# Grid attention in a hybrid diffusion layer: scores, exponentials and scaling as three background steps, and a new order of the steps

## The chip, the cores and the metric

The kernel runs on one core of one Trainium2 chip. The core has a matrix engine (PE, with its weight loads shown apart as PEld), a vector engine (DVE), an activation engine (ACT), a general engine (POOL) and a queue that issues transfers (SP). Each engine works through its own instructions in the order in which the program lists them, and the engines wait for each other on semaphores. The metric is the device time of one execution in microseconds.

## The reference

One layer over 512 latent tokens (an 8 x 64 grid) and 256 context tokens of width 1024. A combined input projection feeds three mixers (a short convolution, a gated linear recurrence, and a neighbourhood attention over the grid), which are merged, projected and followed by a mixture of 16 experts. The change is in the neighbourhood attention, which the reference writes, cut to its core, as

```
s_loc = einsum('bnqhd,bwnkhd->bhnqwk', qr, kr) * scale + bias       # keys of the window
s_ctx = einsum('bnqhd,blhd->bhnql', qr, kc) * scale                 # 256 context keys
p = softmax(concatenate([s_loc, s_ctx], -1), -1)
o = einsum('bhnqwk,bwnkhd->bnqhd', p_loc, vr) + einsum('bhnql,blhd->bnqhd', p_ctx, vc)
```

There are 8 heads and 4 blocks of 16 grid columns. For one head and one block there are 128 queries (8 rows x 16 columns) and 512 keys (256 of the grid, with masked ones at a large negative bias, and 256 of the context).

## The kernel before

**Stages.** The time is spent in a modulation and input projection with the recurrence (to about 386 us), a stage in which the attention is worked off beside the last input projections (about 386 to 561 us), the merge of the branches (561 to 738), the output projection and the router (738 to 828), and the experts, whose 384 MB of weights are streamed from main memory (from 828 to the end).

**The attention is background work.** In its stage the foreground is a list of 128 projection steps of three matmuls each (L453: 128 x 512 outputs, into three PSUM banks named `pj`), and three steps that transpose the last values (`v_rows`, L862 and L868). `weave(fg, bg)` runs the foreground list and after each of its steps takes as many background steps as keep the two lists in proportion by cost. The order of the program is the order of issue: it is written out by hand, and nothing reorders it later. The background list is `att_bg`; an entry `None` is an empty step that only takes its share of the spacing.

**Pairs.** The work is cut into 16 pairs n (a pair of heads, a block of columns); u = 0 and 1 are the two heads. The steps of a pair are:

- `att_scores(n)`: matmuls of queries with grid keys and context keys into two PSUM banks named `hg`, one for each head (L894; there are two such banks in all). On DVE the bias is added (L897) and the maximum of each row is taken (L898). On ACT the exponential with its row sum is taken from PSUM into a buffer `g` in SBUF (L900). In every fourth pair it also issues the three transfers of the next heads' bias (L880).
- `att_scale(n)`: on DVE a reciprocal of the row sum (L908) and the scaling of the probabilities in place (L909).
- `att_turn(n, u)`: four transposes of the scaled probabilities on PE into the one PSUM bank named `tp` (L917), and their copy to SBUF on ACT (L919). The next transposes into `tp` have to wait for that copy.
- `att_values(n)`: matmuls of values with turned probabilities into a bank `acc` (L934); after every fourth pair ACT and DVE split the result into a rounded part and a rest (L939, L940).

**Other work on ACT and DVE.** Each foreground step group also brings casts and differences that split the next weights (L366 on ACT, L367 on DVE), copies out of the `pj` banks (L956 and L994 on ACT), the convolution (L962 to L967 on DVE) and splits of its results (L554, L555). They stand in the same queues.

The list before takes per pair, in this order, values of n-1, scaling of n, scores of n+1 with their exponentials, and the two turns of n.

Of the kernel before, what the change touches and what calls it, by code (L numbers as in the profile page):

```python
# [14 lines left out]
AF = mybir.ActivationFunctionType  # L15
# [131 lines left out]
def mixer_moe(ctx: ExitStack, tc: tile.TileContext, a, out):  # L147
    nc = tc.nc
    V, S, G, PE, SP = nc.vector, nc.scalar, nc.gpsimd, nc.tensor, nc.sync
# [8 lines left out]
    def bank(tag):  # L158
        return psum.tile([128, 512], F32, tag=tag, name=tag, bufs=pbufs[tag])
# [8 lines left out]
    def g512(dt=F32):  # L168
        return gen.tile([128, 512], dt, tag="g", name="g", bufs=NA_)
# [705 lines left out]
    ast = {}  # L875

    def att_load(hp):
        for t in range(3):
            b_ = gen.tile([128, 2, 256], F32, tag="bias", name="bias", bufs=4)
            SP.dma_start(out=b_, in_=a["bias"][2 * hp:2 * hp + 2, :, 256 * t:256 * t + 256].rearrange("u p k -> p u k"))  # L880
            ast["b", hp, t] = b_

    def att_scores(n):
        def f():
            hp, cb = au[n]
            if cb == 3 and hp < 3:
                att_load(hp + 1)
            rs = [slice(64 * u, 64 * u + 64) for u in range(2)]
            ps = [bank("hg") for _ in range(2)]
            qs = nq[hp][:, 128 * cb:128 * cb + 128]  # L890
            for c, keys in enumerate((nk[hp][:, 64 * KB0[cb]:64 * KB0[cb] + 256],
                                      nkc[hp // 2][:, 256 * (hp % 2):256 * (hp % 2) + 256])):
                for u in range(2):
                    PE.matmul(ps[u][:, 256 * c:256 * c + 256], qs[rs[u]], keys[rs[u]], start=True, stop=True)  # L894
            for u in range(2):
                st_ = gen.tile([128, 4], F32, tag="st", name="st", bufs=4)
                V.tensor_tensor(ps[u][:, 0:256], ps[u][:, 0:256], ast["b", hp, BTYPE[cb]][:, u], op=ALU.add)  # L897
                V.tensor_reduce(st_[:, 0:1], ps[u], axis=AX.X, op=ALU.max, negate=True)  # L898
                p = g512()
                S.activation(p, ps[u], AF.Exp, bias=st_[:, 0:1], accum_out=st_[:, 1:2])  # L900
                ast["p", n, u] = (p, st_)
        return f

    def att_scale(n):
        def f():
            for u in range(2):
                p, st_ = ast["p", n, u]
                V.reciprocal(st_[:, 2:3], st_[:, 1:2])  # L908
                V.tensor_scalar(p, p, st_[:, 2:3], None, op0=ALU.mult)  # L909
        return f  # L910

    def att_turn(n, u):
        def f():
            p, _ = ast["p", n, u]
            pt = bank("tp")
            for c in range(4):
                PE.transpose(pt[:, 128 * c:128 * c + 128], p[:, 128 * c:128 * c + 128], ident)  # L917
            pT = g512()
            S.copy(pT, pt)  # L919
            ast["t", n, u] = pT  # L920
            del ast["p", n, u]
        return f

    def att_values(n):
        def f():
            hp, cb = au[n]
            pT = [ast.pop(("t", n, u)) for u in range(2)]
            if cb == 0:
                ast["o"] = bank("acc")
            po = ast["o"]  # L930
            vs = (nv["lat"][:, KB0[cb]], nv["lat"][:, KB0[cb] + 2], nv["ctx"][:, 0], nv["ctx"][:, 1])
            for c in range(4):
                for u in range(2):
                    PE.matmul(po[64 * u:64 * u + 64, 128 * cb:128 * cb + 128],  # L934
                              vs[c][:, 128 * hp + 64 * u:128 * hp + 64 * u + 64],
                              pT[u][:, 128 * c:128 * c + 128], start=(c == 0), stop=(c == 3))
            if cb == 3:
                hi, lo = g512(F32R), g512(F32R)
                S.copy(nat_q(hi), perm_q(po))  # L939
                V.tensor_tensor(nat_q(lo), perm_q(po), nat_q(hi.bitcast(F32)), op=ALU.subtract)  # L940
                yv[2][hp] = (hi, lo)
        return f

    att_bg = [att_scores(0)]
    for n in range(16):
        att_bg += [att_values(n - 1) if n else None, att_scale(n), att_scores(n + 1) if n < 15 else None,
                   att_turn(n, 0), att_turn(n, 1)]
    att_bg += [None, att_values(15)]


    cst = {}
# [172 lines left out]
    for pr in range(2):  # L1124
        for i in (2 * pr, 2 * pr + 1):
            n = 16 + 3 * pr + (i % 2)
            fg += use_item(n, [proj(n, 0, ev_c(i)), proj(n, 1, ev_u(i))])
        n = 18 + 3 * pr
# [371 lines left out]
```

## Time and profile before

| what | us |
|---|---|
| three runs, median (lowest to highest) | 1747.03 (1745.23 to 1747.78) |
| the profiled execution's own time | 1746.03 |
| its span in the trace | 1744.0 |
| attention stage, as the windows below cut it | 174.70 |
| PE busy in it | 154.31 |
| DVE and ACT busy in it | 90.99 and 68.88 |

Four views are read. The windows give each engine's busy time in a stretch, with the clock that PE was granted (1.00 is 2.4 GHz, 0.50 is 1.2 GHz) and the share of time in which the transfer engines were busy. The waits say who stood idle for whom, in total, how often, and the longest. The timeline lists instructions in order of time; a bracket behind one is the idle time of its engine before it and what ended that. The list of transfers gives their size and time to landing. PE's ends are modelled and a new matmul may start before the modelled end of the last one, so distances between starts are read rather than durations.

### The profile page before, as it was taken

To read this page: it belongs to the slowest core of one execution; us is meant where nothing else is said; L and a number is where in the kernel's file an instruction comes from. 1 tells how busy PE (TensorE), PEld (TensorE's weight loads), DVE (VectorE), ACT (ScalarE), POOL (GpSimd) and SP (SyncE) were. 2 spreads that over 40 slices of the span, in tenths; PEclk is the share of its full clock that TensorE was granted. 3 is DMA by queue.
4 is the path that set the end of the run, shared out by engine and by line. 5 is a ranking of instruction groups with operands and counts; after the bars stand their busy time and mean duration, and the time that the engine had idled before them with its cause. 6 is when DMAs were issued, how large, how long until landed. Compare 5 with 4: busy or idle time off the path is not lost.

```text
span 1744.0 us, 20473 instructions
## 1 busy us (share of the span) xinstructions
PE 1616.1 (93%) x8382; PEld 904.6 (52%) x8382; DVE 569.3 (33%) x1135; ACT 369.5 (21%) x759; POOL 79.6 (5%) x150
## 2 busy tenths in 40 slices
PE   4999999998889999999999999898899998989988
PEld 2767888776666888896343342242322322423322
DVE  3518776435554343334012111121121111201211
ACT  3414445333444232323000000000000000000000
POOL 0314330000000000000000000000000000000000
PEclk8999999999999999998999999999999999999999
DMA  9860112111111332355999999999999999999997
GB/s 343 277 245 25 49 49 73 49 67 67 67 61 43 109 133 106 140 226 223 408 426 426 427 426 426 427 427 427 427 426 427 426 427 427 426 427 426 427 426 321
DMA packets 80745, 487.77 MB, mean 280 GB/s; under 512 B 8972, under 2 KB 12556, under 8 KB 25740
## 3 DMA queue, kind: packets, MB, share of 16 engines
q1 hardware_dynamic: 80652, 486.47, 68.3%
q8 instruction: 66, 1.08, 0.2%
q14 instruction: 27, 0.22, 0.0%
HBM read 484.34 MB, written 2.10 MB: 279 GB/s over the span
## 4 chain that ended last, share of the span: by engine, by line
PE 44%; DMA 38%; DVE 6%; ACT 2%; issue 1%; SPq 0%; ACTq 0%; DVEq 0%
PE pj L453 17%; DMA W<-in_w_exp_dram 12%; DMA B<-in_w_exp_dram 9%; PE pj L1365 7%; DMA A<-in_w_exp_dram 7%; DMA D<-in_w_exp_dram 6%; DMA C<-in_w_exp_dram 4%; PE pj L1016 4%; PE acc L1392 3%; PE pj L1197 3%; PE hg L1333 1%; DVE st L898 1%; PE hg L724 1%; PE acc L1437 1%; PE hg L1422 1%
## 5 line engine op out<-in xcount | busy, mean ns | idle before, releaser
L453 PE MATMUL pj<-A,W 128*128 128x512 f32 x1536 | 410.8, 406 | 2.9 <-ACT W L366 1.9
L453 PEld LDWEIGHTS pj<-A,W 128*128 128x128 f32 x1536 | 275.9, 191 | 72.8 <-issue 21.4
L367 DVE TENSOR_TENSOR W<-W 128x512 fp32r<-128x512 f32 (+1 forms) x184 | 122.3, 688 | 166.6 <-ACT W L366 166.4
L1365 PE MATMUL pj<-W,xe 128*64 128x512 f32 x688 | 159.0, 599 | 8.4 <-DMA W<-in_w_exp_dram 8.4
L1425 DVE TENSOR_TENSOR acc<-acc,hg 128x512 f32<-128x512 f32 x120 | 77.1, 684 | 219.2 <-PE hg L1422 219.2
L1372 ACT ACTIVATE s<-pj 128x512 f32<-128x512 f32 x32 | 19.1, 597 | 513.7 <-PE pj L1365 513.7
L1365 PE MATMUL pj<-A,xe 128*64 128x512 f32 x512 | 118.5, 599 | 6.7 <-DMA A<-in_w_exp_dram 6.7
L1365 PE MATMUL pj<-B,xe 128*64 128x512 f32 x432 | 101.3, 599 | 4.2 <-DMA B<-in_w_exp_dram 4.2
L1365 PEld LDWEIGHTS pj<-W,xe 128*64 128x64 f32 x688 | 45.6, 136 | 113.5 <-issue 84.1
L366 ACT CAST W<-W 128x512 fp32r<-128x512 f32 (+1 forms) x184 | 103.3, 599 | 0.0
L1374 DVE TENSOR_TENSOR s<-s,pj 128x512 f32<-128x512 f32 x32 | 21.9, 684 | 231.7 <-PE pj L1365 231.7
L1392 PE MATMUL acc<-W,at 128*64 128x512 f32 x320 | 74.0, 600 | 9.5 <-DMA W<-in_w_exp_dram 9.4
L1413 DVE TENSOR_TENSOR ye<-mod,acc 64x512 f32<-64x512 f32 x30 | 20.6, 686 | 187.0 <-PE acc L1392 186.5
L1365 PEld LDWEIGHTS pj<-A,xe 128*64 128x64 f32 x512 | 33.6, 136 | 83.6 <-issue 62.3
L1382 ACT COPY at<-tp 128x512 f32<-128x512 f32 x32 | 18.8, 586 | 254.8 <-PE tp L1380 254.2
L1422 PE MATMUL hg<-ye,oht 64*128 64x512 f32 x240 | 67.7, 641 | 0.0
L1365 PEld LDWEIGHTS pj<-B,xe 128*64 128x64 f32 x432 | 28.5, 136 | 69.8 <-issue 54.5
L1392 PE MATMUL acc<-B,at 128*64 128x512 f32 x240 | 56.5, 600 | 8.0 <-DMA B<-in_w_exp_dram 8.0
L453 PEld LDWEIGHTS pj<-C,W 128*128 128x128 f32 x384 | 59.0, 190 | 9.1 <-ACT y L625 0.8
L1365 PE MATMUL pj<-C,xe 128*64 128x512 f32 x256 | 59.0, 597 | 4.1 <-DMA C<-in_w_exp_dram 4.1
L453 PE MATMUL pj<-C,W 128*128 128x256 f32 x384 | 61.4, 282 | 0.0
L1333 PEld LDWEIGHTS hg<-ot,xn 128*128 128x128 f32 x512 | 59.1, 195 | 2.7 <-issue 2.7
(287 smaller groups left out, 1775.1 us busy)
## 6 DMA issues: line engine op xcount, KB each, us to landing
W<-in_w_exp_dram SPq DMA_DIRECT2D x126, 1024.0 KB, 19.5
A<-in_w_exp_dram SPq DMA_DIRECT2D x88, 1024.0 KB, 19.6
B<-in_w_exp_dram SPq DMA_DIRECT2D x85, 1024.0 KB, 19.6
C<-in_w_exp_dram SPq DMA_DIRECT2D x42, 1024.0 KB, 19.6
D<-in_w_exp_dram SPq DMA_DIRECT2D x42, 1024.0 KB, 19.6
W<-in_w_in_dram SPq DMA_DIRECT2D x34, 1024.0 KB, 4.8
y<-in_w_mod_dram SPq DMA_DIRECT2D x32, 256.0 KB, 6.0
g<-in_w_mod_dram SPq DMA_DIRECT2D x32, 256.0 KB, 5.4
```

Of the source, the lines that this page charges most:

```text
L366: S.copy(hi[:, sl], raws[n][:, sl])
L367: V.tensor_tensor(lo[:, sl], raws[n][:, sl], hi[:, sl].bitcast(F32), op=ALU.subtract)
L453: PE.matmul(dst, w[wi][:, k, 128 * b:128 * b + 128], src[xi][:, k], start=(k == 0 and p == 0), stop=(k == KT - 1 and p == 2))
L1016: PE.matmul(st["p"], wb[wi][:, 4 * br + k], yv[br][k][xi], start=(k == 0 and p == 0), stop=(k == 3 and p == 2))
L1197: PE.matmul(st["p"][:, 256 * u:256 * u + 256], mm[k][mi][:, ts], w[wi][:, k], start=(k == 0 and p == 0), stop=(k == KT - 1 and p == 2))
L1333: PE.matmul(px[:, 128 * k:128 * k + 128], xn[:, i, 128 * kk:128 * kk + 128], ot[:, 128 * i:128 * i + 128], start=(i == 0), stop=(i == 3))
L1365: PE.matmul(pg[64 * u:64 * u + 64], xp[:, kk, 64 * (e % 2):64 * (e % 2) + 64], wt[:, k, 512 * u:512 * u + 512], start=(kk == 0), stop=(kk ...
L1374: V.tensor_tensor(est["s", j], est["s", j], pg, op=ALU.mult)
L1392: PE.matmul(est["y"][64 * u:64 * u + 64], lhs, wt[:, k, 512 * u:512 * u + 512], start=(kk == 0), stop=(kk == 15))
L1413: V.tensor_tensor(ye[us], mod5[us, 512 * u:512 * u + 512], y[us], op=ALU.mult)
L1422: PE.matmul(pc, oht[64 * u:64 * u + 64, 128 * i:128 * i + 128], ye[64 * u:64 * u + 64], start=True, stop=True)
L1425: V.tensor_tensor(av, av, pc, op=ALU.add)
```

## The change

`att_scores(n)` is cut in two. What is left of it ends with the row maximum on DVE and notes the PSUM bank and the small tile with the maximum. A new step `att_exp(n)` takes the exponentials on ACT. Scaling, turns and values are unchanged in themselves, but the list is written in another order with more empty steps. Before, it had 83 entries, five for a pair; now it has 134, eight for a pair: scores of n+1, first turn of n, values of n-1, second turn of n, exponentials of n+1, an empty step, scaling of n+1, an empty step.

```
                 V.tensor_reduce(st_[:, 0:1], ps[u], axis=AX.X, op=ALU.max, negate=True)
+                ast["s", n, u] = (ps[u], st_)
+        return f
+
+    def att_exp(n):
+        def f():
+            for u in range(2):
+                ps, st_ = ast.pop(("s", n, u))
                 p = g512()
-                S.activation(p, ps[u], AF.Exp, bias=st_[:, 0:1], accum_out=st_[:, 1:2])
+                S.activation(p, ps, AF.Exp, bias=st_[:, 0:1], accum_out=st_[:, 1:2])
                 ast["p", n, u] = (p, st_)
...
-    att_bg = [att_scores(0)]
+    att_bg = [att_scores(0), None, None, None, att_exp(0), None, att_scale(0), None]
     for n in range(16):
-        att_bg += [att_values(n - 1) if n else None, att_scale(n), att_scores(n + 1) if n < 15 else None,
-                   att_turn(n, 0), att_turn(n, 1)]
-    att_bg += [None, att_values(15)]
+        att_bg += [att_scores(n + 1) if n < 15 else None, att_turn(n, 0), att_values(n - 1) if n else None,
+                   att_turn(n, 1)]
+        att_bg += [att_exp(n + 1), None, att_scale(n + 1), None] if n < 15 else [None, att_values(15)]
```

On PE this is one pair in the middle of the stage, from the scores of pair 9 to those of pair 10, before the change. The tile names are those of the section on the kernel; `x6` is a count of matmuls as the program lists them.

```order
L894 MATMUL hg<-g 128x256 x4
L453 MATMUL pj<-A,W 128x512 x6
L917 MATMUL tp<-ident,g 128x128 x4
L453 MATMUL pj<-A,W 128x512 x3
L917 MATMUL tp<-ident,g 128x128 x4
L453 MATMUL pj<-A,W 128x512 x6
L934 MATMUL acc<-g,nvl 64x128 x4
L934 MATMUL acc<-g,nvc 64x128 x4
L453 MATMUL pj<-A,W 128x512 x9
L894 MATMUL hg<-g 128x256 x4
```

The two turns (L917) stand with three or six projection matmuls between them. On the same stretch of PE the changed program lists this (its L924 is the old L917, its L941 the old L934):

```order
L894 MATMUL hg<-g 128x256 x4
L453 MATMUL pj<-A,W 128x512 x3
L924 MATMUL tp<-ident,g 128x128 x4
L453 MATMUL pj<-A,W 128x512 x3
L941 MATMUL acc<-g,nvl 64x128 x4
L941 MATMUL acc<-g,nvc 64x128 x4
L453 MATMUL pj<-A,W 128x512 x3
L924 MATMUL tp<-ident,g 128x128 x4
L453 MATMUL pj<-A,W 128x512 x15
L894 MATMUL hg<-g 128x256 x4
```

The values of the pair before now stand between the two turns, and 15 projection matmuls stand between the second turn and the next scores.

On ACT these are the exponentials of pair 9 and what follows to those of pair 10, before the change:

```order
L900 ACTIVATE g,st<-hg,st 128x512 x2
L919 COPY g<-tp 128x512
L366 CAST W<-W 128x512
L919 COPY g<-tp 128x512
L956 COPY g<-pj 128x512
L366 CAST W<-W 128x512
L900 ACTIVATE g,st<-hg,st 128x512 x2
```

Both copies of turned probabilities of pair 8 (L919) stand behind the two exponentials of pair 9. In the changed program this is ACT from the exponentials of pair 8 to those of pair 9 (its L907 is the old L900, L926 the old L919, L946 the old L939, L963 the old L956):

```order
L907 ACTIVATE g,st<-hg,st 128x512 x2
L366 CAST W<-W 128x512 x2
L926 COPY g<-tp 128x512
L946 CAST g<-acc 128x512
L963 COPY g<-pj 128x512
L926 COPY g<-tp 128x512
L366 CAST W<-W 128x512
L907 ACTIVATE g,st<-hg,st 128x512 x2
```

Both copies of pair 8 now stand ahead of the exponentials of pair 9.

## Rows read from the trace of the kernel before

**Rows 1.** Windows: stretch, its length, PE, PEld, DVE, ACT, POOL busy, clock, DMA.

```profile
386.50:561.20 174.70, 154.31 (x931) 111.97 (x929) 90.99 (x189) 68.88 (x147) 0.00 (x0) 0.98 0.18 59
561.20:738.00 176.80, 176.80 (x782) 145.88 (x783) 68.86 (x112) 54.59 (x105) 10.30 (x8) 1.00 0.31 113
1011.00:1603.00 592.00, 540.82 (x2529) 186.94 (x2524) 99.42 (x185) 38.69 (x70) 0.00 (x0) 1.00 1.01 427
```

**Rows 2.** Waits in 386.5 to 561.2: us in total, times, longest.

```profile
ACT g L900 <- DVE st L898: 68.2, 31, 5.7
...
PE tp L917 <- ACT g L919: 16.4, 14, 2.3
...
PE tp L862 <- ACT nvl L864: 2.1, 1, 2.1
...
PE tp L917 <- ACT nvc L869: 1.9, 1, 1.9
```

**Rows 3.** Timeline of pair 9: start, length, engine, line, tiles, count, idle before.

```profile
482.28 1.13 PE L894 MATMUL hg<-g 64*128 64x256 f32 x8
...
483.16 0.49 DVE L909 TENSOR_SCALAR g<-g,st 128x512 f32<-128x512 f32 x1
...
483.35 1.66 PE L453 MATMUL pj<-A,W 128*128 128x512 f32 x6
...
483.75 0.49 DVE L909 TENSOR_SCALAR g<-g,st 128x512 f32<-128x512 f32 x1
...
485.20 0.95 PE L453 MATMUL pj<-A,W 128*128 128x512 f32 x3
...
486.03 0.69 ACT L900 ACTIVATE g<-hg,st 128x512 f32<-128x512 f32 x1 [4.28 <-DVE st L898]
...
486.28 0.69 DVE L898 TENSOR_REDUCE st<-hg 128x1 f32<-128x512 f32 x1
...
487.09 0.69 ACT L900 ACTIVATE g<-hg,st 128x512 f32<-128x512 f32 x1 [0.28 <-DVE st L898]
...
487.77 0.57 ACT L919 COPY g<-tp 128x512 f32<-128x512 f32 x1
...
488.39 0.66 PE L917 MATMUL tp<-ident,g 128*128 128x128 f32 x4 [2.25 <-ACT g L919]
...
490.36 0.66 PE L934 MATMUL acc<-g,nvl 128*64 128x128 f32 x8
...
491.38 2.33 PE L453 MATMUL pj<-A,W 128*128 128x512 f32 x9
...
493.64 1.13 PE L894 MATMUL hg<-g 64*128 64x256 f32 x8
```

**Rows 4.** Timeline of PE around the first turn after the scores of pair 14.

```profile
536.36 0.96 PE L453 MATMUL pj<-A,W 128*128 128x512 f32 x3
537.16 0.60 PE L917 MATMUL tp<-ident,g 128*128 128x128 f32 x4
537.52 1.64 PE L453 MATMUL pj<-A,W 128*128 128x512 f32 x6
```

**Rows 5.** Timeline of the turns of pair 15, which no scores follow.

```profile
556.10 0.60 PE L917 MATMUL tp<-ident,g 128*128 128x128 f32 x4
...
556.78 0.59 ACT L919 COPY g<-tp 128x512 f32<-128x512 f32 x1 [2.18 <-PE tp L917]
557.42 0.42 PEld L917 LDWEIGHTS tp<-ident,g 128*128 128x128 f32 x4 [0.46 <-ACT g L919]
557.42 0.66 PE L917 MATMUL tp<-ident,g 128*128 128x128 f32 x4
```

**Rows 6.** Windows at the start of the stage, columns as in rows 1.

```profile
394.00:396.00 2.00, 0.88 (x5) 0.40 (x3) 1.06 (x3) 1.59 (x5) 0.00 (x0) 1.00 0.00 0
396.00:398.00 2.00, 0.99 (x6) 0.77 (x6) 1.42 (x5) 0.96 (x2) 0.00 (x0) 1.00 0.00 0
398.27:411.88 13.61, 11.76 (x58) 8.38 (x57) 5.24 (x12) 4.62 (x10) 0.00 (x0) 0.76 0.11 29
```

**Rows 7.** Transfers of the bias, and the expert weights' queue waiting (561 to 1100).

```profile
bias<-in_bias_dram SPq DMA_DIRECT2D x12, 256.0 KB, 5.2
...
SPq L1055 <- PE pj L1197: 16.4, 2, 16.0
```

## The prediction, written before the changed kernel had run

> **What bounds the kernel now.** I read the windows by stage first. In the attention stage PE is busy for 154.31 of 174.70 us, so it stands idle for 20.4 us, while in the merge behind it PE is busy for all of 176.80 us [rows 1]. DVE and ACT are busy for 90.99 and 68.88 us there, and the transfer engines for 0.18 of the time. None of these three is near its limit, so what the stage loses is lost to order, not to work.
>
> The waits then say whose order. All of PE's idle time is three groups: 16.4 us in 14 waits of a turn (L917) for the copy of the turn before it, 1.9 us of a turn for a copy in front of it, and 2.1 us of the value transposes (L862) for their copy. Sum 20.4 us. The largest wait of the stage is not PE's: ACT stands 68.2 us in front of its exponentials (L900) for the row maximum on DVE [rows 2].
>
> The timeline ties the two together. In pair 9 ACT idles 4.28 us, takes the first exponential at 486.03, the second at 487.09, and only then, at 487.77, the copy out of `tp`. Those transposes had long been done; the projection matmuls behind them started at 485.20. The next turn starts at 488.39, after 2.25 us of PE idle [rows 3]. So ACT's queue is the wait: the copies stand behind exponentials that are not ready. Where no exponentials stand in the way, behind the last scores, the turn starts at 556.10, its copy at 556.78, and the next turn at 557.42: 1.32 us from turn to turn, and PE lists no idle time there, only its weight load 0.46 us [rows 5].
>
> What follows the stage shifts with it. The merge is all PE. The experts are bound by transfers (share 1.01 from 1011 to 1603 us, [rows 1]), but their stream begins when PE frees the buffers: the queue's loads of expert weights waited 16.4 us for matmuls of the output projection (L1197) [rows 7]. A us saved before that is a us saved at the end, since the stream starts earlier and is as long.
>
> **The change part by part.** No instruction is added or removed on any engine; the same matmuls, copies and exponentials come in another order.
>
> *The waits removed.* The copies of pair n now stand ahead of the exponentials of n+1 on ACT. A first turn's copy needs 1.32 us until the second turn can start [rows 5]. Between the two starts there are now the step from turn to projection (0.36, from 537.16 to 537.52), three projection matmuls (0.80, from 536.36 to 537.16, [rows 4]), the values (1.02, from 490.36 to 491.38, [rows 3]) and three more matmuls (0.80): 2.98 us. The slack is 1.7 us, enough for two more ACT steps of the copy's size (0.57). So 16.4 + 1.9 us go. The 2.1 us of the value transposes go too, since their copy now stands ahead of the first exponentials; a rest is counted below.
>
> *What the listed waits leave out.* In pair 9 the three matmuls start at 485.20 and the turn would follow at 486.00 (0.80 later, [rows 4]); it came at 488.39. That is 2.39 us lost where 2.25 is listed, because an idle time counts from a modelled end that the next matmul would not have waited for. 0.14 us for each of 17 waits (14, 1 and 1 are listed in [rows 2], and one shows on a weight load alone, [rows 5]): 2.4 us.
>
> *The clock.* From 394 to 398 us, where the first exponentials held up the first copies, PE was busy for 0.88 and 0.99 of two times 2 us. The 13.61 us behind that were granted 0.76 of the full clock, that is a part of them at 1.2 in place of 2.4 GHz [rows 6]. 0.24 x 13.61 = 3.3 us. The bounds of this term are 0 (the fall has another cause or comes elsewhere) and 3.3. I take 3.3, because the merge, where PE has no gaps, was granted 1.00 throughout [rows 1], and the gaps ahead of the fall are among those that go.
>
> *New waits on PE.* (a) Value transposes: three matmuls between two of them, 0.36 + 0.80 = 1.16 against 1.32 needed: 0.16 us, once. The third group of them waits for a copy on DVE behind the row maxima of pair 0: about 0.1. (b) The last values now stand three matmuls behind the last turn, where nine stood: again 1.16 against 1.32, 0.16 us. (c) Scores need both `hg` banks back, which the later exponentials hold longer. From the second turn the copy ends after 0.68 + 0.59 = 1.27 us [rows 5], one exponential takes 0.68 us from start to start (487.09 to 487.77) and the second is done 0.69 after its start [rows 3]: 1.27 + 0.68 + 0.69 = 2.64 us. PE meanwhile has 0.36 us and 15 matmuls. Nine took 2.26 (491.38 to 493.64), so 15 take some 3.6 to 3.8: the scores come 4.0 us after the turn. Slack 1.3 us, enough for two steps of the copy's size; 0 by this, up to 0.5 a pair if the queue holds more. (d) The exponentials must find the maxima ready. In pair 9 the last maximum is done at 486.97, 4.7 us after the scores started at 482.28, although scalings stood ahead of it. The changed order comes to the exponentials 1.07 (482.28 to 483.35) + 0.80 + 2.98 + 1.27 = 6.1 us after the scores. ACT's 68.2 us of waiting shrinks to little. (e) A first turn needs its scaling. Exponentials end 2.64 us after the second turn; scaling takes 0.59 a half (483.16 to 483.75), some 1.3 us with the reciprocals; 4.0 us. The next first turn comes at 4.0 + 1.07 + 0.80 = 5.9, or 5.1 in the two pairs that have no matmul between scores and turn. Slack over 1 us. Sum of new waits: 0.4 us.
>
> *What else moves.* The bias transfers go with the scores; they land in 5.2 us [rows 7] and are wanted one pair later, some 9 us: nothing. DVE now waits at the scaling for the exponentials, and behind it stand weight differences and the convolution; these have a projection step group of slack each, and cost nothing unless (c) or (e) slip.
>
> Sum: 16.4 + 1.9 + 2.1 + 2.4 + 3.3 - 0.4 = 25.7 us. The profiled execution took 1746.03 us (span 1744.0 and 2.0 around it), so 1720.3. It lies 1.0 below the median of the runs and inside them (1745.23 to 1747.78); half of that added, I say 1720.5.
>
> **The rivals.** *The wait moves to the `hg` banks or the scaling.* For it: both chains are longer than before, and ACT and DVE carry casts and evacuations between the steps that I counted. Against it: the slacks of over 1 us. If a pair loses 0.5 us, 15 pairs lose 7.5: 1728.
>
> *The clock does not come back, or falls elsewhere.* The waits go, the 3.3 us stay: 1723.8.
>
> *The one bank is the limit.* One could say that the gap at each second turn is there because the one `tp` bank is too few; then the order would change nothing, and the time would be 1746. Against it stand the turns of pair 15: the same bank, 1.32 us, no listed idle time [rows 5]. A rule of the Trainium skill goes that way: Perfetto Trace Analysis, Optimization Strategy, says that a gap which repeats on the engine that should be saturated can mean that there isn't enough SBUF or PSUM for the next tile. By it the 14 waits would stay here; the trace disagrees, by the rows of pair 15. The same result would come if the experts' stream didn't start earlier; the wait for L1197 speaks against it.
>
> *A ring through two queues, slower.* First turn, copy, second turn, copy, exponentials, scaling and the next first turn now form one ring: 1.32 + 1.27 + 1.37 + 1.3 = 5.3 us, against a pair of some 9 (11.36 - 2.39 in pair 9, [rows 3]). Before, the exponentials overlapped with the turns. If casts, evacuations and the convolution all fell into the ring in each pair, about five steps on ACT of 0.6 and six on DVE of 0.6, it would be 5.3 + 6.6 = 11.9 us, 2.9 above the free pair. Fifteen times that is 44 against the 25.7 gained: 1764. It is slower from about 10.7 us on, that is when nine such steps stand in the ring in every pair; the listed order has two or three there.
>
> **How the numbers follow.** My forecast, between 1717.5 and 1723.0, has 0.70. The clock rival has 0.06, the moved wait (1723 to 1734) 0.15, no change 0.04, slower 0.03, and a gain larger than all the terms 0.02. The low end takes the sum of 26.1 without new waits and the spread of the runs below the profile (0.8) with some 1.5 for small distances that I rounded: 1717.5. The high end takes in the clock case and about half of the moved waits: 1727.0; 0.02 + 0.07 + 0.07 stay outside. Differences under 0.2% (3.5 us) can't be told from no change here. Faster 0.93, same 0.04, slower 0.03.
>
> **What would show it.** In the changed profile PE's waits for the copies should be under 1 us in sum, where 18.3 stood; ACT's wait for the row maximum should be some us, not 68; the copies should start about 0.7 us after their turn; the stage should last about 149 us at a clock of 1.00; the merge should begin about 26 us earlier and all later stages keep their length. A wait of L894 for the exponentials would mean the first rival, a wait of a first turn for the scaling the last; a window under 1.00 in the stage the second. A DMA stream that begins at the old time would make the prediction wrong altogether.

## The result and the profile after

The changed kernel took 1720.18 us (median; 1719.64 to 1721.72), the kernel before in the same comparison 1747.18 (1745.23 to 1747.78). The ratio is 0.9855, with a 95% interval of 0.9844 to 0.9867: 27.0 us less, where 1720.5 us had been predicted. The profiled execution took 1719.64 us with a span of 1717.5.

The windows by stage come first, with the columns of [rows 1]. In the changed kernel the attention stage ends some 27 us earlier.

```profile
386.50:534.70 148.20, 147.84 (x931) 110.92 (x930) 91.69 (x190) 67.14 (x148) 0.00 (x0) 1.00 0.21 70
534.70:711.50 176.80, 176.80 (x787) 145.98 (x786) 68.85 (x113) 54.60 (x106) 10.30 (x8) 1.00 0.32 115
```

PE is busy for 147.84 of 148.20 us, where it was 154.31 of 174.70, and its clock is 1.00 in place of 0.98 [rows 1]. The idle time left is 0.4 us. DVE and ACT do as much work as before. The merge behind it is all PE, as before.

For a length that doesn't depend on where a window is cut, I take the start of the last long group of projections ahead of the scores of pair 0 (nine matmuls of L453 from `C`), and the start of the first 36 matmuls of the merge. These two are, from the timeline and from the chain that ended last of the changed kernel:

```profile
388.49 1.24 PE L453 MATMUL pj<-C,W 128*128 128x256 f32 x9
...
533.91 8.48 PE pj L1023 x36
```

The stage is 145.42 us long by them; before, the same two starts stand at 389.15 and 561.20, which is 172.05. The stage has lost 26.6 us. What lies behind it takes 1717.5 - 533.91 = 1183.6 us, and took 1744.0 - 561.20 = 1182.8: the gain of the stage is the gain of the kernel.

The waits of the stage, with the columns of [rows 2] (us in total, times, longest):

```profile
ACT g L926 <- PE tp L924: 63.5, 28, 3.9
...
DVE st L915 <- ACT g L907: 5.2, 4, 1.9
...
PE tp L924 <- DVE st L915: 0.4, 1, 0.4
...
PEld hg L894 <- ACT g L907: 0.4, 1, 0.4
```

PE's three groups of [rows 2] are gone. ACT's wait of 68.2 us for the row maxima (L898) is gone too, and 63.5 us stand in another place: ACT now idles in front of the copies, for the turns of PE. That is idle time which costs nothing, since PE is the bound and runs through. One wait of PE is left, 0.36 us of the first turn of pair 15 for its scaling.

The timeline shows how a pair runs now, from the scores of pair 2 to those of pair 3:

```profile
404.82 1.13 PE L894 MATMUL hg<-g 64*128 64x256 f32 x8
...
406.70 0.60 PE L924 MATMUL tp<-ident,g 128*128 128x128 f32 x4
...
407.33 0.59 ACT L926 COPY g<-tp 128x512 f32<-128x512 f32 x1 [3.90 <-PE tp L924]
...
407.93 0.66 PE L941 MATMUL acc<-g,nvl 128*64 128x128 f32 x8
...
409.74 0.60 PE L924 MATMUL tp<-ident,g 128*128 128x128 f32 x4
...
410.38 0.59 ACT L926 COPY g<-tp 128x512 f32<-128x512 f32 x1 [1.94 <-PE tp L924]
...
410.86 0.62 ACT L366 CAST W<-W 128x512 fp32r<-128x512 f32 x1
411.38 0.69 ACT L907 ACTIVATE g<-hg,st 128x512 f32<-128x512 f32 x1
...
412.06 0.69 ACT L907 ACTIVATE g<-hg,st 128x512 f32<-128x512 f32 x1
...
413.73 1.13 PE L894 MATMUL hg<-g 64*128 64x256 f32 x8
```

The first copy starts 0.63 us after its turn does, at 407.33, and is done at 407.92; the second turn comes at 409.74 and finds its bank free. In pair 9 before, the copy started at 487.77, 2.57 us after the projections behind its turn, and PE stood [rows 3]. The second exponential ends at 412.75, and the next scores, which need the two banks that the exponentials read, come at 413.73: 0.98 us later, which I call the slack. In the 15 pairs this slack is 0.03 to 1.76 us, with a median of 0.96.

### The profile page after: what moved, and what is told of

Its sections match the earlier page's. It is cut to its first block, busy times and chain, and to the rows that moved or that the text cites. A ratio compares the mean times of both kernels' runs of the same rounds, so it can differ in the third digit from the quotient of the medians.

```text
span 1717.5 us, 20477 instructions
## 1 busy us (share of the span) xinstructions
PE 1610.1 (94%) x8382; PEld 903.4 (53%) x8382; DVE 569.8 (33%) x1135; ACT 367.6 (21%) x759; POOL 79.7 (5%) x150
## 2 busy tenths in 40 slices
DMA packets 80745, 487.77 MB, mean 284 GB/s; under 512 B 8972, under 2 KB 12556, under 8 KB 25740
## 4 chain that ended last, share of the span: by engine, by line
PE 50%; DMA 37%; DVE 4%; ACT 1%; issue 0%; SPq 0%; DVEq 0%; ACTq 0%
PE pj L453 19%; DMA W<-in_w_exp_dram 11%; DMA B<-in_w_exp_dram 9%; PE pj L1372 8%; DMA A<-in_w_exp_dram 7%; DMA D<-in_w_exp_dram 5%; DMA C<-in_w_exp_dram 5%; PE pj L1023 4%; PE acc L1399 4%; PE pj L1204 3%; PE hg L1340 2%; PE hg L1429 1%; PE hg L894 1%; PE acc L941 1%; PE hg L724 1%; PE tp L924 1%
## 5 line engine op out<-in xcount | busy, mean ns | idle before, releaser
L453 PE MATMUL pj<-A,W 128*128 128x512 f32 x1536 | 408.6, 405 | 2.9 <-ACT W L366 1.9
L453 PEld LDWEIGHTS pj<-A,W 128*128 128x128 f32 x1536 | 274.8, 190 | 71.9 <-issue 21.0
L453 PEld LDWEIGHTS pj<-C,W 128*128 128x128 f32 x384 | 59.1, 190 | 9.1 <-ACT y L625 0.8
L453 PE MATMUL pj<-C,W 128*128 128x256 f32 x384 | 61.6, 283 | 0.0
```

What stands on the lines that cost most here:

```text
L453: PE.matmul(dst, w[wi][:, k, 128 * b:128 * b + 128], src[xi][:, k], start=(k == 0 and p == 0), stop=(k == KT - 1 and p == 2))
```

## The experiments

The change does two things at once. It moves the exponentials of pair n+1 behind the copies of pair n on ACT (order), and it puts the values between the two turns, with three projection matmuls on either side, so that a turn and the next stand further apart (distance: by the sum of the prediction 2.98 us of PE work from the first turn to the second, and 3.04 in pair 2 above, in place of 1.16 where three matmuls stood and some 1.8 where six did). My theory was the order; the rivals were the distance, the one `tp` bank, and for the size of the gain the clock and the slack of the new ring. The kernels, with the length of the stage by the two starts named above. A ratio is to the kernel before of the same comparison. A length of the stage comes from one profiled execution, while the times of one kernel lie up to 4 us apart (copies first: 1723.06 to 1727.19), so small differences between two lengths are readings of single executions.

| kernel | us (median) | ratio to before, 95% | stage, us |
|---|---|---|---|
| before | 1747.18 beside the changed kernel, 1745.91 (e1 to e4) and 1745.51 (e5 to e7) beside the experiments | 1 | 172.05 |
| changed kernel | 1720.18 | 0.9855 (0.9844 to 0.9867) | 145.42 |
| copies first, old list (e1) | 1725.24 | 0.9882 (0.9868 to 0.9897) | 150.92 |
| new list, exponentials with scores (e2) | 1725.47 | 0.9882 (0.9867 to 0.9897) | 150.84 |
| second bank alone (e3) | 1732.33 | 0.9926 (0.9910 to 0.9943) | 157.86 |
| new order in the first pair, 14 entries (e4) | 1750.26 | 1.0029 (1.0017 to 1.0041) | 176.6 |
| new order in the first pair, old list (e6) | 1738.81 | 0.9962 (0.9947 to 0.9977) | 165.10 |
| e1 with the exponentials of pair 0 later (e7) | 1722.55 | 0.9868 (0.9853 to 0.9883) | 147.50 |
| changed kernel, 2 more copies per pair on ACT (e5) | 1727.75 | 0.9899 (0.9882 to 0.9915) | 152.36 |
| changed kernel, 4 more copies per pair on ACT (e5) | 1744.04 | 0.9992 (0.9983 to 1.0001) | 169.36 |

### Order alone: copies ahead of the exponentials, old list

The functions are the changed ones; the list is that of before, with the exponentials put into the entry of the second turn (`both` runs its arguments one after the other):

```diff
-    att_bg = [att_scores(0), None, None, None, att_exp(0), None, att_scale(0), None]
+    att_bg = [both(att_scores(0), att_exp(0))]
     for n in range(16):
-        att_bg += [att_scores(n + 1) if n < 15 else None, att_turn(n, 0), att_values(n - 1) if n else None,
-                   att_turn(n, 1)]
-        att_bg += [att_exp(n + 1), None, att_scale(n + 1), None] if n < 15 else [None, att_values(15)]
+        att_bg += [att_values(n - 1) if n else None, att_scale(n), att_scores(n + 1) if n < 15 else None,
+                   att_turn(n, 0), both(att_turn(n, 1), att_exp(n + 1)) if n < 15 else att_turn(n, 1)]
+    att_bg += [None, att_values(15)]
```

> The list of before with its 83 entries and its distances; only the two exponentials of pair n+1 are moved from the scores' entry to behind the second turn of n, so the copies stand ahead of them on ACT. The exponentials of pair 0 stay where they were. Theory (order on ACT): PE's waits of a turn for a copy fall from 18.3 us to under 2 (a second turn only three matmuls behind the first comes 0.16 us too early); the 2.1 us of the value transposes stay, and the fall of the clock behind them may stay (3.3 us). Time 19 to 22 us below before, 1725 to 1728. Rival (distance between the two turns is what counts): the distances are those of before, so most of the 16.4 us stay and the time is within 5 us of before.

It took 1725.24 us, and its stage is 21.1 us shorter than before. Of PE's waits one is left; all 16.4 us of the turns have gone, and the 1.9 us of the turn behind the copy of L869.

```profile
PE tp L862 <- ACT nvl L864: 2.1, 1, 2.1
```

At the start of the stage pair 0's exponentials still stand right behind its scores. The clock falls there again, for 0.27 x 4 + 0.16 x 4 = 1.7 us by the windows, where the same sum gave 3.3 before:

```profile
396.00:400.00 4.00, 3.16 (x14) 1.95 (x14) 2.28 (x6) 0.79 (x2) 0.00 (x0) 0.73 0.00 0
400.00:404.00 4.00, 4.00 (x22) 3.37 (x21) 2.75 (x5) 1.85 (x4) 0.00 (x0) 0.84 0.00 0
```

So the order alone takes away the idle time at the second turns, with no entry added and no distance changed. Of the 21.1 us, 1.9 (the copy of L869) and 1.6 (the clock) belong to the start and not to the second turns.

### Distance alone: the new list, exponentials with the scores

```diff
-    att_bg = [att_scores(0), None, None, None, att_exp(0), None, att_scale(0), None]
+    sc = lambda n: both(att_scores(n), att_exp(n))
+    att_bg = [sc(0), None, None, None, None, None, att_scale(0), None]
     for n in range(16):
-        att_bg += [att_scores(n + 1) if n < 15 else None, att_turn(n, 0), att_values(n - 1) if n else None,
+        att_bg += [sc(n + 1) if n < 15 else None, att_turn(n, 0), att_values(n - 1) if n else None,
                    att_turn(n, 1)]
-        att_bg += [att_exp(n + 1), None, att_scale(n + 1), None] if n < 15 else [None, att_values(15)]
+        att_bg += [None, None, att_scale(n + 1), None] if n < 15 else [None, att_values(15)]
```

> The new list with its 134 entries, the values between the two turns, but the exponentials back in the scores' entry, so that the first copy stands behind the next pair's exponentials as before. Theory (order on ACT alone): the waits stay, time within 5 us of before. Rival (distance): in the trace of before a first copy starts 4.2 to 5.5 us after the scores; the second turn now comes 4.85 us after them, so at most 1.3 us of wait a pair is left and in most pairs none: listed waits for copies 2 to 8 us, time 1723 to 1731.

It took 1725.47 us: the rival was right here, and the expectation of the order theory, that the gaps stay, fell. The waits of this kernel:

```profile
ACT g L907 <- DVE st L898: 65.6, 31, 5.2
...
PE tp L924 <- ACT g L926: 3.5, 6, 1.4
...
PE tp L862 <- ACT nvl L864: 1.4, 1, 1.4
```

ACT waits for the row maxima as long as before (65.6 us), and the copies stand behind the exponentials as before. In its timeline one pair reads:

```profile
463.65 0.60 PE L924 MATMUL tp<-ident,g 128*128 128x128 f32 x4
...
464.20 0.69 ACT L907 ACTIVATE g<-hg,st 128x512 f32<-128x512 f32 x1 [4.43 <-DVE st L898]
...
465.27 0.69 ACT L907 ACTIVATE g<-hg,st 128x512 f32<-128x512 f32 x1 [0.29 <-DVE st L898]
...
465.94 0.58 ACT L926 COPY g<-tp 128x512 f32<-128x512 f32 x1
...
466.72 0.60 PE L924 MATMUL tp<-ident,g 128*128 128x128 f32 x4
```

The copy comes 2.29 us after its turn, behind both exponentials, but PE's own work puts the second turn 3.07 us behind the first, and PE doesn't wait.

This list spaces out the start too, so it is not a test of the second turns alone. The value transposes wait 1.4 us in place of 2.1, the wait for the copy of L869 is gone, and the clock stays at 1.00 there:

```profile
396.00:400.00 4.00, 3.06 (x16) 2.09 (x16) 2.82 (x7) 1.79 (x4) 0.00 (x0) 1.00 0.00 0
400.00:404.00 4.00, 3.76 (x21) 2.60 (x21) 2.39 (x5) 1.40 (x4) 0.00 (x0) 1.00 0.00 0
```

By the listed waits and the windows, 2.6 us of waits and 3.3 of clock of its 21 are the start's, and 12.9 us are waits of the turns (16.4 to 3.5). So there are two ways to most of one gain. Each alone takes 21 us from the stage; together they take 26.6.

### A second bank, all else as before

```diff
     def att_turn(n, u):
         def f():
             p, _ = ast["p", n, u]
-            pt = bank("tp")
+            pt = bank("pj" if u else "tp")
```

> The kernel before, list and all, with one edit: the second turn of a pair goes into one of the three pj banks, so it needs no copy to be done. If the one tp bank alone is the limit, the 16.4 us go and the time is 16 to 20 us below before. If the late copies are what costs, the wait moves to the values of the same pair, which stand one entry behind the second turn and need both copies: about 1 us a pair there, time 4 to 12 us below before. The 2.1 and 1.9 us at the start stay in both.

It took 1732.33 us, between the two expectations: the stage is 14.2 us shorter (390.46 to 548.32), about half of what the change brings. Some 1.6 us of that is the clock at the start: 0.95 and 0.62 in the two stretches of 4 us from 396 to 404 are 1.7 us, in place of 3.3. Its waits (lines of the kernel before: L934 values, L919 copy):

```profile
PEld acc L934 <- ACT g L919: 10.6, 22, 0.9
...
PE acc L934 <- ACT g L919: 3.6, 8, 0.6
...
PE tp L862 <- ACT nvl L864: 2.1, 1, 2.1
...
PE tp L917 <- ACT nvc L869: 1.7, 1, 1.7
```

The second turns no longer wait for the first turns' copies. But the copies are as late as before, and now the values wait for them: a part of the wait moved one step down. The projections, which lend the bank, have no listed wait of PE. I had weighed a rule against the change: the Trainium skill, Perfetto Trace Analysis, Optimization Strategy, says that a gap that repeats on the engine to be saturated can mean too little SBUF or PSUM. The traces agree by half. A second bank for the turns takes about half of the gain (14.2 of 26.6 us), while the first two experiments take most of it (21) with the one bank.

### The clock at the start: the first pair in the new order

[rows 6] showed PE's clock at 0.76 for 13.6 us behind an idle time of 2.1 us at 395 to 397, and I had priced that at 3.3 us. To see this apart from the rest, pair 0 alone gets the new order. In the first kernel for this the start has 14 entries in place of 6:

```diff
-    att_bg = [att_scores(0)]
-    for n in range(16):
-        att_bg += [att_values(n - 1) if n else None, att_scale(n), att_scores(n + 1) if n < 15 else None,
+    att_bg = [att_scores(0), None, None, None, att_exp(0), None, att_scale(0), None,
+              att_scores(1), att_turn(0, 0), None, att_turn(0, 1), att_exp(1), None]
+    for n in range(1, 16):
+        att_bg += [att_values(n - 1), att_scale(n), both(att_scores(n + 1), att_exp(n + 1)) if n < 15 else None,
                    att_turn(n, 0), att_turn(n, 1)]
```

> Pair 0 and the scores of pair 1 in the new order, all later pairs in the order of before. It asks for the clock term. If the gaps at the start cause the fall of the clock, 2.1 + 1.9 us of waits, some 0.3 hidden with them and 3.3 us of clock go: 7 to 8 us below before, with a clock of 1.00 from 394 to 412 us. If the fall has another cause, 4 to 5 us, and the clock still falls there. The waits of the later turns stay near 15 us in both.

It took 1750.26 us, 4.4 more than before, where 7 to 8 less was expected. The experiment mixed two things. The list has 8 entries more than before, and since the entries are spread over the same projections, they come denser: between the turns of the later pairs there is less to do. The turns' waits grew to 22.7 us, and the clock fell later on:

```profile
PE tp L924 <- ACT g L926: 22.7, 14, 3.8
```

```profile
392.00:412.00 20.00, 19.89 (x111) 14.94 (x111) 12.78 (x27) 7.91 (x18) 0.00 (x0) 1.00 0.23 80
412.00:420.00 8.00, 5.87 (x31) 4.20 (x30) 4.13 (x11) 3.63 (x8) 0.00 (x0) 0.95 0.10 33
420.00:430.00 10.00, 9.05 (x51) 6.24 (x51) 4.28 (x8) 2.42 (x6) 0.00 (x0) 0.87 0.29 105
...
480.00:490.00 10.00, 8.20 (x39) 6.15 (x41) 3.20 (x7) 4.32 (x9) 0.00 (x0) 0.66 0.01 2
```

The start itself is clean (1.00 from 392 to 412), as expected, but the falls in the three windows under 1.00 come to 0.05 x 8 + 0.13 x 10 + 0.34 x 10 = 5.1 us, more than the 3.3 saved. In the last of them PE stood idle for some 1.2 us with the clock already down, which leaves about 4.5. The listed waits are 2.8 us longer (23.2 against 20.4) and the clock's loss is 1.2 to 1.8 greater: 4.0 to 4.6, where the stage is 4.6 us longer. The longest of the idle times stands right ahead of the last fall, in the timeline:

```profile
481.80 1.12 PE L924 MATMUL tp<-ident,g 128*128 128x128 f32 x4 [3.77 <-ACT g L926]
```

Four transposes take 1.12 us there where they take 0.60 to 0.66 elsewhere. So a second pair of kernels was made that leaves the list's length and the distances alone. In the first, pair 0's exponentials go one entry later (into the empty entry), and those of pair 1 behind the second turn of pair 0:

```diff
+        sc = att_scores(n + 1) if n == 0 else both(att_scores(n + 1), att_exp(n + 1)) if n < 15 else None
-        att_bg += [att_values(n - 1) if n else None, att_scale(n), att_scores(n + 1) if n < 15 else None,
-                   att_turn(n, 0), att_turn(n, 1)]
+        att_bg += [att_values(n - 1) if n else att_exp(0), att_scale(n), sc, att_turn(n, 0),
+                   both(att_turn(n, 1), att_exp(1)) if n == 0 else att_turn(n, 1)]
```

> The list of before with its 83 entries and distances. Only at the start the exponentials of pair 0 come one entry later (behind the first value transposes) and those of pair 1 behind the second turn of pair 0; all later pairs as before. It asks for the clock term without changing the spacing of the rest. The waits at the start fall from 4.0 to about 1 us, those of the later turns stay near 16. If the gaps at the start cause the fall of the clock, 3.3 us more come back: 6 to 7 us below before, 1739 to 1740, and the clock is 1.00 from 394 to 412 us. If the clock falls anyway, 3 us below before.

It took 1738.81 us, 6.7 less than before, as expected. The clock stays at 1.00 over the stretch in which it was 0.76, and the waits of the later turns stay:

```profile
394.00:412.00 18.00, 16.98 (x110) 12.39 (x110) 10.81 (x24) 9.49 (x23) 0.00 (x0) 1.00 0.30 103
```

```profile
PE tp L924 <- ACT g L926: 16.3, 14, 2.2
```

The stage is 6.95 us shorter; 4.1 of that are listed idle time (20.4 to 16.3), and the other 2.85 are the clock together with what two listed waits fewer (14 in place of 16) leave out. The second does the same to the kernel with the order alone:

```diff
-    att_bg = [both(att_scores(0), att_exp(0))]
+    att_bg = [att_scores(0)]
     for n in range(16):
-        att_bg += [att_values(n - 1) if n else None, att_scale(n), att_scores(n + 1) if n < 15 else None,
+        att_bg += [att_values(n - 1) if n else att_exp(0), att_scale(n), att_scores(n + 1) if n < 15 else None,
...
```

> The kernel with the old distances and all copies ahead of the exponentials, with one edit: the exponentials of pair 0 come one entry later too. In that kernel the clock fell to 0.73 and 0.84 in 396 to 404 us behind one wait of 2.1 us, a loss of 1.7 us. If the gap causes the fall, the wait shrinks to about 1 us, the clock stays at 1.00 and the time falls by some 3 us to 1722, 2 us above the changed kernel (turns three matmuls apart). If not, it falls by about 1 us.

It took 1722.55 us with no listed idle time of PE and a clock of 1.00:

```profile
394.00:412.00 18.00, 17.90 (x116) 12.98 (x114) 11.68 (x26) 9.35 (x23) 0.00 (x0) 1.00 0.29 103
```

Its stage is 3.4 us shorter than that of the order alone: 2.1 of listed idle time and 1.3 beside it, where 0.27 x 4 + 0.16 x 4 = 1.7 was lost to the clock. Still 2.1 us longer than the changed kernel, with nothing listed on PE. What is listed is weight loads that wait for the copies:

```profile
PEld tp L924 <- ACT g L926: 3.2, 7, 0.5
```

Between the turns of this kernel stand six matmuls at most, 1.8 us. In the seven pairs with three matmuls the copy is just late: the second turn starts 1.33 us behind the first (1.27 in one of them), where the matmuls alone make it 1.16, and that is 1.1 us in sum. With 2.98 us between the turns these waits are gone as well. So of the 5.5 us between the order alone and the changed kernel, 3.4 are the later exponentials of pair 0 and 1.1 the distance; the runs don't split the last 1.0.

### The ring: more work for ACT ahead of the exponentials

The rival on the other side was a ring through ACT and DVE that becomes longer than a pair. The changed kernel gets two, then four copies of 128x512 in each pair, which nobody uses:

```diff
     def att_exp(n):
         def f():
+            for _ in range(2):
+                S.copy(g512(), nv["lat"][:, 0])
             for u in range(2):
```

> The changed kernel with two extra copies of 128 x 512 from SBUF to SBUF on ACT in front of each pair's exponentials (their result is used by nobody). It asks how much slack the later exponentials have before the next scores wait for their hg banks. In the changed kernel's trace the second exponential ends 2.5 us after the second turn, 3.0 with a weight cast in front of it, and the scores start 3.96 us after that turn. Two copies cost 1.0 to 1.2 us of ACT: theory (slack of 1 to 1.5 us) expects a wait of scores under 0.3 us in a few pairs and a time within 2 us of the changed kernel. If the slack were already used up, each of 15 pairs would lose about 1 us: 1735.

Two copies a pair took the stage from 145.42 to 152.36 us, 6.9 more, where under 2 was expected. The slack was smaller than I had worked out. The waits tell little of it; the timeline tells more:

```profile
PEld hg L894 <- ACT g L909: 5.9, 13, 0.8
...
PE tp L926 <- DVE st L917: 1.7, 1, 1.7
PE hg L894 <- ACT g L909: 1.1, 3, 0.4
```

```profile
439.30 1.15 ACT L905 COPY g<-nvl 128x512 f32<-128x512 f32 x2
...
441.01 0.69 ACT L909 ACTIVATE g<-hg,st 128x512 f32<-128x512 f32 x1
...
441.18 1.80 PE L894 MATMUL hg<-g 64*128 64x256 f32 x8 [0.42 <-ACT g L909]
```

The scores of the next pair begin when the first exponential has let its bank go, and their second half waits for the second exponential inside the group: the row is 1.80 us long in place of 1.13. These 0.67 us are not listed as idle time. In ten of the 15 pairs the row is longer than 1.3 us; what these have above 1.13 comes to 4.2 us, and with the listed 1.7 and 1.1 that is the 6.9. The 1.7 is not a wait of scores: it is the first turn of pair 15, which waits for its scaling.

> As the run with two, with four extra copies: 2.0 to 2.4 us of ACT in each pair. Theory: the slack of 1 to 1.5 us is gone, the scores wait 0.6 to 1.2 us for the exponentials in each of 15 pairs, time 9 to 18 us above the changed kernel, 1729 to 1738. If ACT has slack everywhere (it is busy for less than half of the stage), no loss: 1720.

Four copies a pair took the stage to 169.36 us, 23.9 more than in the changed kernel (9 to 18 expected), and the time to 1744.04, the time of before within 0.2%. The step from two to four costs (169.36 - 152.36) / 15 = 1.13 us a pair, and two copies more take 2.18 - 1.15 = 1.03 us on ACT: past the slack, ACT's time is paid about in full. Waits and one pair of this kernel:

```profile
PEld hg L894 <- ACT g L909: 20.7, 30, 2.1
PE hg L894 <- ACT g L909: 8.7, 10, 1.7
...
PE tp L926 <- DVE st L917: 2.5, 1, 2.5
```

```profile
443.68 2.18 ACT L905 COPY g<-nvl 128x512 f32<-128x512 f32 x4
...
446.43 0.69 ACT L909 ACTIVATE g<-hg,st 128x512 f32<-128x512 f32 x1
...
446.59 1.80 PE L894 MATMUL hg<-g 64*128 64x256 f32 x8 [1.67 <-ACT g L909]
```

So the ring exists, and it closes at the `hg` banks: scores, first turn, values, second turn, copy, exponentials, and back to the scores. Only in pair 15, behind which no scores stand, is it a turn that waits for its scaling.

## Why the prediction was right, and where its steps were not

- **What bounds the kernel** was right. PE ran through the stage once the waits had gone, the merge began 27.3 us earlier (0.7 of it because this run came to the stage earlier), and the stages behind kept their length within 0.8 us: nothing was given back to the transfers.
- **The waits removed** (16.4 + 1.9 + 2.1): 20.4 us of idle time became 0.4. Right in size. As for the cause, I put it down to the order on ACT alone; the experiment on the distance showed a second sufficient one. The 2.98 us that I worked out between the two turns were in my slack, but not seen as a reason of their own, and I did not ask what the same list would do with the copies left behind the exponentials.
- **What the listed waits leave out and the clock** (2.4 + 3.3 = 5.7): the stage lost 26.6 us, 20.0 of them listed, so the two and everything else are worth 6.6. The sum was 0.9 too low. The first-pair experiment on the old list gives the clock and two waits' hidden part together 2.85; less 2 x 0.14 that is 2.6. So the clock is worth 2.6 to 2.9 rather than 3.3, and 3.7 to 4.0 are left for the hidden part in place of 2.4, some 0.2 us a wait. These runs don't split the two more finely. What I read as one fall of 13.61 us was two (last section), the second behind the wait for the copy of L869, and both are gone with their waits.
- **The sum and the forecast.** That the time came within 0.3 us of the forecast is partly luck. The sum of 25.7 was 0.9 below what the stage lost and 1.3 below the 27.0 between the medians: the hidden part was 1.3 to 1.6 too low, the clock 0.4 to 0.7 too high. The last step also has a slip: 1720.3 with half of 1.0 added is 1720.8, not 1720.5.
- **New waits** (0.4): 0.36 us is listed, at another place than I had named. The value transposes and the last values show no idle time of PE; the one wait is the first turn of pair 15 for its scaling, the one I had called covered by over 1 us.
- **The slack of the scores, step (c)**, was mis-sized. I had 1.3 us in each pair, enough for two more steps of the copy's size. The second exponential ends 3.01 us after the second turn in pair 2, not 2.64, because a cast of weights stands between copy and exponentials (0.52 from its start to theirs); other pairs have more there. In the pair with the least slack it is a cast (L554) that itself waits 0.83 us for DVE. The slack is 0.03 to 1.76 us. It held in all pairs, so the term's cost of 0 stood; but two more steps cost 6.9 us.
- **The ring rival** had its length wrong, and was further from impossible than I said. I took 1.32 us from first to second turn; PE's own order makes that 3.04 (406.70 to 409.74), and I left out the 1.88 from the scores to the first turn. With these, the ring up to the next scores is 1.88 + 3.04 + 1.23 (turn and copy) + 1.37 (two exponentials) = 7.5 us, and 7.9 with the cast, against a pair of 8.9: four more steps on ACT in each pair take the whole gain, not nine.
- **The bank rival** was put too low as a mechanism: a second bank is worth some 12.6 us of the stage (14.2 with the clock). That the order would change nothing for lack of a bank was wrong, as I said; the turns of pair 15 [rows 5] had shown it.
- **The moved wait and the clock that doesn't come back** did not occur: 0.4 us listed for the scores' weight load, and a clock of 1.00 throughout the stage.

No other order that was run is better than the changed kernel. PE has 0.4 us of listed idle time left there, so little more is to be expected from the order of this stage; no run shows what its unlisted waits still hold.

## What to carry to other kernels

When the bounding engine idles a little in every round of a loop, look at the queue of the engine that it waits for: a ready instruction behind one that isn't ready yet is a wait with two cures, to issue the ready one first, or to give the waiting engine more of its own work in between; here either took most of it, and they didn't add up. Before moving steps later, walk the whole ring with the bounding engine's own steps in it, and count every cast and eviction that the queue holds: the slack is that of the worst pair, not of the cleanest one. In an experiment on one pair of a list that is spread over other work, keep the list's length, or all the other distances change with it.

## What was unexpected of the hardware

The clock did not go by the length of the idle time alone. In the 13.6 us of [rows 6] it fell twice, each time behind an idle time of PE. In the six stretches of 2 us from 398 to 410 it was 0.51, 0.64, 1.00, 0.71, 0.50 and 0.93, and these two rows stand ahead of the falls:

```profile
397.01 0.55 PE L862 MATMUL tp<-ident,g 128*128 128x128 f32 x3 [2.14 <-ACT nvl L864]
...
403.80 0.66 PE L917 MATMUL tp<-ident,g 128*128 128x128 f32 x4 [1.85 <-ACT nvc L869]
```

The 2.25 us ahead of 488.39 [rows 3] brought no such fall. In the kernel with 14 entries 2.13 us ahead of 418.06 and 3.77 us ahead of 481.80 brought one (0.87 over 420 to 430, 0.66 over 480 to 490), and 3.09 us ahead of 506.06 brought none (1.00 over 500 to 510). What else decides it the runs don't show.

A wait of PE inside a group of matmuls shows as a longer row (1.80 us in place of 1.13) and not as idle time, and one that a weight load takes shows on PE's weight loads alone: two kernels with no PE idle time, or 0.4 us of it, differ by 2.1 us in the stage. So a sum of listed waits is a lower end.
